# Two Winograd products of each SwiGLU pair in matmuls of 512 columns, and later operands for the last product

## The chip, the cores and the metric

The kernel runs on one core of one Trainium2 chip. The time is the device time of one execution in microseconds, as the median of several runs. Engines are named as in the profile: PE is TensorE's matmul, PEld its weight load, DVE VectorE, ACT ScalarE, POOL GpSimd, SP SyncE (which issues most DMAs).

## The reference

A decoder block on x of 512 tokens by 1024, in float32: two token mixers side by side, a sigmoid-gated merge, and a SwiGLU channel mixer with D_FF = 2816.

```
h  = rmsnorm(x, norm1_g);  z = h @ w_in + b_in
ya = conformer_conv(z) @ conv_w_out + conv_b_out
yb = (rg_lru(z) * gelu(z_rg)) @ lru_w_out
x  = x + (sigmoid(z_ga)*ya + sigmoid(z_gb)*yb) @ w_mix_out
h  = rmsnorm(x, norm2_g)
x  = x + (silu(h @ ffn_w1) * (h @ ffn_w3)) @ ffn_w2
out = rmsnorm(x, norm_f_g)
```

The change lies in the line before the last.

## The kernel before, in words

Every float32 operand of a large product is split into a high and a low part (`split`: ACT casts the high part, L123, DVE or POOL subtracts it from the original, L119). A product then is three matmuls: high weights by high tokens, high by low, low by high. A tile is 128 partitions by 512 columns.

The FFN's first two matrices run in 11 pairs k of 128-row blocks of D_FF (k and k + 11). Pair 0 is computed plainly; for pairs 1 to 10 the 2×2 blocks (block of D_FF by block of D_MODEL, by half of the tokens) go through a seven-product form of Winograd's: b11, t1, b21, t2, t4, b22 and t3. Each product is one call of `f_product` (L1082): for w1 and then w3 (`HALVES[i]` of one PSUM bank), for four blocks c, the three matmuls of 256 token columns, so 24 matmuls. The token operands stand in `f_in` (a11, s1 and so on, each as a pair of high and low parts of 256 columns), the weights in chunks of 128x1024 (`hl_fb`, `hl_ft` in the profile: plain blocks and sums). `ffn_product` calls it and combines: b11 goes into bank `fa`, which ACT copies to `fb` (L1182), b21 then accumulates into `fb` and t2 into `fa`; t1 goes into bank `fe` of another pool, which ACT copies to the tile `se` (L1187) and DVE adds after b22 and t3 (L906). `f_out` makes silu(w1 part) times w3 part (L1147, L1148) into the tiles `ou` and `ov`. The t1, t2, t3 sums of weights are made on DVE (L357, L119), t4's by an accumulating DMA of POOL (L355). The first two b11/b21 products of pairs 1 to 4 run earlier (`FIRST`, `NEXT`).

`F_ORDER` sets the order of the products, and with it the order in which weight chunks are loaded and split; `weights` works four chunks ahead of PE (`AHEAD`), with five buffers of split weights and four of raw ones. Within that a scheduler fixes the order of the instructions on each engine when the program is built.

The last product (w2, `Sevenfold` with name "o", tiles `or`, L953) has the same form in 512-column matmuls. `pair(k)` prepares its token operands from `ou` and `ov` of pair k: a split of u (`ous`), a sum s1 and its split (`os1p`), and two more operands, `oe` and the overwritten `ov`. `run` has a first part (products r1, r2, r5 over all k), in which `oe` and `ov` are also split (`oeb`, `ovb`), a second part (r7, r1 and r3 over all k), and a third part. At the end of the first part DVE adds the finished products to the residual (`plus`, tiles `x2b`). `SUMS_FROM` sets from which t4 on `pair` is called inside the FFN: with 5, after t4 of pairs 5 to 10, for pairs 0 to 5.

Of the kernel before, what the change touches and what calls it, by code (L numbers as in the profile page):

```python
# [8 lines left out]
F32 = mybir.dt.float32  # L9
F32R = mybir.dt.float32r  # L10
AF = mybir.ActivationFunctionType
# [21 lines left out]
SLOTS, SHORT, GATES = 59, 5, 6  # L33
# [11 lines left out]
PLAIN, FIRST, NEXT = 0, (1, 2), (3, 4)  # L45
BEGUN = FIRST + NEXT
ADDING = ()
SUMS_FROM, SUMS_AHEAD = 5, 3
GATES_AT = 6
SEED_AT = 4  # L50
SUMS_AT, SUMS_STEP, SUMS_LAG, STORE_LAG = 4, 3, 2, 4


# [33 lines left out]
def tile_block(ctx, tc, a, out):  # L87
    nc = tc.nc
# [12 lines left out]
    longt, shortt, gatet = tiles("long", SLOTS), tiles("short", SHORT), tiles("gate", GATES)  # L101
# [5 lines left out]
    def bank(name):  # L107
        return psum.tile([P, T], F32, tag="mm", name=name)

    def bank2(name):  # L110
        return psum2.tile([P, T], F32, tag="cv", name=name)

    vec, act, pe, pool_e = nc.vector, nc.scalar, nc.tensor, nc.gpsimd
# [4 lines left out]
    def sub(eng, o, x, y):  # L118
        return eng.tensor_tensor(out=o, in0=x, in1=y, op=ALU.subtract)  # L119
# [13 lines left out]
    def split(name, full, eng, p_=None, copy=act.copy):  # L133
        p_ = p_ or pairt(name)
        return split_to(*p_, full, eng, copy)[:2]
# [48 lines left out]
    def weights(key, ahead=AHEAD):  # L184
        i = next(i for i, c in enumerate(chunks) if c[0] == key)
        emit_to(i + 1 + ahead)
        return held.pop(key)
# [144 lines left out]
    KF = NF // 2  # L332
# [70 lines left out]
    F_PAIRS = [k for k in range(KF) if k != PLAIN]  # L403
    F_ORDER = []
    for k, before in zip(F_PAIRS, [None] + F_PAIRS):
# [2 lines left out]
            F_ORDER.append(("t4", before))  # L408
        F_ORDER += [("b22", k), ("t3", k)]
    F_ORDER.append(("t4", F_PAIRS[-1]))  # L410
    for n, k in F_ORDER:
        f_chunk(n, k)
    outq = Quartered("o", a["ffn_w2"][0].rearrange("(k p) n -> p k n", p=P), NF // 2, vec)
# [78 lines left out]
    eps_t = consts.tile([P, 1], F32, name="eps_t")  # L492
    vec.memset(eps_t, EPS)
    warm = consts.tile([P, 1], F32, name="warm")
# [102 lines left out]
    HALVES = [slice(0, 256), slice(256, 512)]  # L597
# [293 lines left out]
    for j in range(8):  # L891
        ws = w_tiles(f"lo{j}_0", 5) + w_tiles(f"lo{j}_1", 5)
        ps = bank(f"yb{j}")
# [12 lines left out]
    add = lambda o, x, y: vec.tensor_tensor(out=o, in0=x, in1=y, op=ALU.add)  # L906
    LO, HI = HALVES
# [7 lines left out]

    class Sevenfold:
        def __init__(self, q):
            self.q, self.uv, self.ops = q, {}, {}
            self.name, self.kh = q.name, q.kh

        def tile(self, j, make):
# [9 lines left out]
        def pair(self, k):  # L931

            n = self.name
            if k in self.ops:
                return
            ua, va = self.uv[k]
            u_ = split(f"{n}us{k}", ua, vec)
            s1 = shortt(f"{n}s1{k}")[:, LO]
            add(s1, va[:, LO], va[:, HI])
            sp = longt(f"{n}s1p{k}", F32R)  # L940
            split_to(sp[:, LO], sp[:, HI], s1, vec)
            e = (gatet if n == "o" and k < GATES else longt)(f"{n}e{k}")
            sub(vec, e[:, HI], ua[:, LO], va[:, LO])
            sub(vec, va[:, LO], s1, ua[:, LO])
            sub(vec, e[:, LO], ua[:, HI], va[:, LO])
            self.ops[k] = u_, sp, e, va

        def product(self, banks, i, x_, w_, start, stop, again=False):

# [5 lines left out]
        def run(self, sums, begun, end):  # L955

            n, kh, get = self.name, self.kh, self.q.get  # L960
            quarter = lambda p_, cs: tuple(v[:, cs] for v in p_)
            plus = lambda t, h, b_: add(sums[t][h], b_, sums[t][h])
            late = []
            r1, r2, r5 = ([bank(f"{n}{r}{i}") for i in range(2)] for r in ("r1", "r2", "r5"))
            for k in range(kh):
                for kk in range(min(kh, k + 1 + SUMS_AHEAD)):
                    self.pair(kk)
                wb21, wb11, wt1 = get(k, "b21", "b11", "t1")
                u_, sp, e, va = self.ops[k]
                todo = [(r1, quarter(u_, LO), wb11), (r2, quarter(u_, HI), wb21), (r5, (sp[:, LO], sp[:, HI]), wt1)]  # L970
                ends = k == kh - 1
                order = [(r, i) for i in range(2) for r in (0, 1)] + [(2, 0), (2, 1)] if ends else [(r, i) for r in range(3) for i in range(2)]
                for r, i in order:
                    self.product(todo[r][0], i, *todo[r][1:], k == 0, ends)
                    if ends and r == 1:
                        plus(i, 0, r1[i])
                        plus(i, 0, r2[i])
                late.append((split(f"{n}eb{k}", e, vec), split(f"{n}vb{k}", va, vec)))
                if k == 0:
                    begun()  # L980
            r2, r7 = [bank(f"{n}r3{i}") for i in range(2)], [bank2(f"{n}r7{i}") for i in range(2)]

            def second(k, wb22, wt2, wt3):
                e, va = late[k]
                todo = [(r7, quarter(e, HI), wt3), (r1, quarter(va, LO), wt2), (r2, quarter(e, LO), wb22)]
                ends = k == kh - 1
                order = [(r, i) for i in range(2) for r in (1, 2)] + [(0, 0), (0, 1)] if ends else [(r, i) for r in range(3) for i in range(2)]
                for r, i in order:
                    self.product(todo[r][0], i, *todo[r][1:], r != 1 and k == 0, ends, r == 1)

            def third(i, ks, cols=None):
                for dst, cs in cols or [(r1[i], slice(0, T))]:
                    for k in ks:
                        (wh, wl), = get(k, "t4")
                        self.product({i: dst}, i, quarter(late[k][1], HI), (wh[:, cs], wl[:, cs]), False, k == kh - 1, True)

            for k in range(kh - 1):
                second(k, *get(k, "b22", "t2", "t3"))
                if k == 0:
                    for i in range(2):  # L1000
                        plus(i, 1, r5[i])
                        plus(2 + i, 1, r5[i])

            act.activation(warm, late[-1][1][0][:, :1].bitcast(F32), AF.Sqrt, scale=0.0, bias=eps_t)
            last = get(kh - 1, "b22", "t2", "t3", ahead=AHEAD - 1)
            end(lambda: second(kh - 1, *last), plus, r1, r2, r7, third)

    m7 = Sevenfold(mixq)
    for n, j in enumerate(mixq.order()):
        ws = w_tiles(f"co{j}", ND)  # L1010
        ps = bank(f"ya{j}")
        mm3(ps, ws, un)
        o = sga[j]
# [56 lines left out]
    o7 = Sevenfold(outq)  # L1070
# [5 lines left out]
    def f_product(ps, k, x_, w_, again=False, ahead=AHEAD):  # L1076

        h, l = weights(f"f{w_}_{k}", ahead)
        for i in range(2):
            for c, (xh, xl) in enumerate(x_):  # L1080
                for m, (lw, rx_) in enumerate(((h, xh), (h, xl), (l, xh))):
                    pe.matmul(  # L1082
                        ps[:, HALVES[i]], lw[:, 4 * i + c, :], rx_, start=not (again or i or c or m),
                        stop=bool(i and c == 3 and m == 2), skip_group_check=True,
                    )

    first = {}
    for k in FIRST:
# [11 lines left out]
    with tc.manual_schedule(engines={ET.PE}):  # L1100
        ws = w_tiles(f"f1_{PLAIN}", ND, 0)
        for q in range(4):
            cs, ks = HALVES[q // 2], range(4 * (q % 2), 4 * (q % 2) + 4)
# [60 lines left out]
    for k in NEXT:  # L1164
        f_product(first[k][1], k, f_in["a12"], "b21", True)
        o7.uv[k] = longt(f"ou{k}"), longt(f"ov{k}")
        f_out(first[k][1], o7.uv[k][0][:, LO])

    seven = {}

    def ffn_product(n, k):

        b_ = seven.setdefault(k, {"a": first[k][0]} if k in BEGUN else {})
        x_ = {"b11": "a11", "b21": "a12", "b22": "s4", "t1": "s1", "t2": "s2", "t3": "s3", "t4": "a22"}[n]
        r = {"b11": "a", "b21": "b", "b22": "a", "t1": "e", "t2": "a", "t3": "c", "t4": "c"}[n]
        if n in ("b11", "t1"):
            b_[r] = (bank2 if r == "e" else bank)(f"f{r}_{k}")
        ps = b_[r]
        f_product(ps, k, f_in[x_], n, n not in ("b11", "t1"))
        if n in ("b11", "t2"):  # L1180
            new = b_["b" if n == "b11" else "c"] = bank(f"f{n}_{k}")
            act.copy(new, ps)  # L1182
            if n == "b11":
                o7.uv[k] = longt(f"ou{k}"), longt(f"ov{k}")
        elif n == "t1":
            b_["se"] = shortt(f"se_{k}")
            act.copy(b_["se"], ps)  # L1187
        elif n == "b22":
            add(ps, ps, b_["se"])
        elif n == "t3":  # L1190
            newest["added"] = add(b_["se"], ps, b_["se"]).ins
        if n not in ("b11", "t1", "t2"):
            i, cs = {"b21": (0, LO), "b22": (0, HI), "t3": (1, HI), "t4": (1, LO)}[n]
            f_out(b_["se"] if n == "t3" else ps, o7.uv[k][i][:, cs], -1.0 if n in ("b22", "t3") else 1.0)
        if n == "t4" and k >= SUMS_FROM:
            o7.pair(k - SUMS_FROM)

    for n, k in F_ORDER:
        ffn_product(n, k)

    x2 = [[longt(f"x2b{t}{h}") for h in range(2)] for t in range(NT)]
# [100 lines left out]
```

## Time and profile before

| | |
|---|---|
| runs | 797.24, 797.38, 797.41 us; median 797.38 |
| profiled execution | 797.4 us, span 795.6 us |
| granted TensorE clock | 1.0 |
| PE busy | 789.3 us (99%), 4378 matmuls |
| DVE busy | 673.9 us (85%) |
| ACT busy | 472.2 us (59%) |
| POOL busy | 229.2 us (29%) |

Times are in microseconds from the start of the span. Busy shares are shares of the span; the duration that a row gives for a matmul reaches into the next one, so the rate is read from start to start, or from the chain of work that ended last. The FFN's seven-product stage reaches from about 480 to 686 us, the last product from there to 790 us.

### The profile page before, as it was taken

To read this page: it belongs to the slowest core of one execution; us is meant where nothing else is said; L and a number is where in the kernel's file an instruction comes from. 1 tells how busy PE (TensorE), PEld (TensorE's weight loads), DVE (VectorE), ACT (ScalarE), POOL (GpSimd) and SP (SyncE) were. 2 spreads that over 40 slices of the span, in tenths; PEclk is the share of its full clock that TensorE was granted. 3 is DMA by queue.
4 is the path that set the end of the run, shared out by engine and by line. 5 is a ranking of instruction groups with operands and counts; after the bars stand their busy time and mean duration, and the time that the engine had idled before them with its cause. 6 is when DMAs were issued, how large, how long until landed. Compare 5 with 4: busy or idle time off the path is not lost.

```text
span 795.6 us, 12203 instructions
## 1 busy us (share of the span) xinstructions
PE 789.3 (99%) x4378; PEld 691.2 (87%) x4378; DVE 673.9 (85%) x1024; ACT 472.2 (59%) x686; POOL 229.2 (29%) x181
## 2 busy tenths in 40 slices
PE   9999999999999999999999999999999999999997
PEld 8888888888888888888888898999999999888886
DVE  6699899999989988786887889978878887889757
ACT  6646585988768855563335475545555555577434
POOL 1855766797666855130000000000000000000000
PEclk9999999999999999999999999999999999999999
DMA  6944647487555664468947545567555553676652
GB/s 204 259 137 144 192 138 209 121 243 211 169 172 172 206 189 120 129 201 278 280 140 245 172 134 158 129 170 188 152 133 133 133 133 106 202 269 204 195 176 106
DMA packets 184604, 140.29 MB, mean 176 GB/s; under 512 B 14259, under 2 KB 162143, under 8 KB 184543
## 3 DMA queue, kind: packets, MB, share of 16 engines
q1 hardware_dynamic: 183103, 134.27, 55.8%
q0 software_dynamic: 1440, 5.24, 3.5%
q8 instruction: 34, 0.56, 0.3%
q14 instruction: 27, 0.22, 0.1%
HBM read 113.79 MB, written 18.64 MB: 166 GB/s over the span
## 4 chain that ended last, share of the span: by engine, by line
PE 98%; DVE 1%; issue 0%; ACT 0%; ACTq 0%
PE z L534 36%; PE or L953 12%; PE ft L1082 7%; PE yb L534 7%; PE fa L1082 7%; PE fr L1082 6%; PE ya L534 5%; PE mxr L953 5%; PE fe L1082 4%; PE g L827 3%; PE fb L1082 2%; PE f L534 2%; PE warm L506 1%; PE f L1108 1%; PE tx L574 1%; PE th L574 0%
## 5 line engine op out<-in xcount | busy, mean ns | idle before, releaser
L702 DVE SCALAR_TENSOR_TENSOR cv<-u,par,cv 128x511 f32<-128x511 f32 (+19 forms) x240 | 162.6, 733 | 5.7 <-ACT cv L699 5.4
L119 POOL TENSOR_TENSOR hl_in<-raw_in,hl_in 128x1024 fp32r<-128x1024 f32 x51 | 123.6, 2427 | 82.9 <-ACT hl_in L123 69.4
L355 POOL DMA_DIRECT2D raw_fb<-raw_fb x10 | 8.7, 875 | 298.3 <-DVE raw_fb L357 186.2
L119 POOL TENSOR_TENSOR ows<-ows 128x256 f32<-128x256 f32 x66 | 57.0, 866 | 37.4 <-DMA ows<-in_ffn_w_dram 34.4
L123 ACT CAST hl_ft<-raw_fb 128x1024 fp32r<-128x1024 f32 x40 | 41.9, 1049 | 32.1 <-DVE raw_fb L357 16.6
L123 ACT CAST hl_in<-raw_in 128x1024 fp32r<-128x1024 f32 x50 | 52.1, 1043 | 11.2 <-PE z L534 6.6
L119 DVE TENSOR_TENSOR hl_ft<-raw_fb,hl_ft 128x1024 fp32r<-128x1024 f32 x40 | 48.6, 1221 | 6.6 <-ACT hl_ft L123 6.5
L119 DVE TENSOR_TENSOR hl_fb<-raw_fb,hl_fb 128x1024 fp32r<-128x1024 f32 x30 | 36.6, 1222 | 9.4 <-ACT hl_fb L123 9.2
L357 DVE TENSOR_TENSOR raw_fb<-raw_fb,raw_fb 128x1024 f32<-128x1024 f32 x20 | 24.5, 1225 | 20.9 <-DMA raw_fb<-in_ffn_w_dram 20.5
L534 PE MATMUL z<-h10h,hl_in 128*128 128x512 f32 (+1 forms) x108 | 41.5, 385 | 0.0
L534 PE MATMUL z<-h17h,hl_in 128*128 128x512 f32 (+1 forms) x108 | 41.1, 381 | 0.0
L534 PE MATMUL z<-h13h,hl_in 128*128 128x512 f32 (+1 forms) x108 | 41.1, 381 | 0.0
L534 PE MATMUL z<-h15h,hl_in 128*128 128x512 f32 (+1 forms) x108 | 41.1, 381 | 0.0
L534 PE MATMUL z<-h14h,hl_in 128*128 128x512 f32 (+1 forms) x108 | 41.1, 381 | 0.0
L534 PE MATMUL z<-h16h,hl_in 128*128 128x512 f32 (+1 forms) x108 | 41.1, 381 | 0.0
L534 PE MATMUL z<-h12h,hl_in 128*128 128x512 f32 (+1 forms) x108 | 41.1, 381 | 0.0
L534 PE MATMUL z<-h11h,hl_in 128*128 128x512 f32 (+1 forms) x108 | 41.1, 381 | 0.0
L123 ACT CAST hl_fb<-raw_fb 128x1024 fp32r<-128x1024 f32 x30 | 31.4, 1047 | 8.6 <-PE mxr L953 3.7
L119 DVE TENSOR_TENSOR hl_ob<-raw_ob,hl_ob 128x1024 fp32r<-128x1024 f32 (+1 forms) x23 | 27.1, 1178 | 9.8 <-ACT hl_ob L123 7.0
L123 ACT CAST hl_ob<-raw_ob 128x1024 fp32r<-128x1024 f32 (+1 forms) x23 | 23.3, 1014 | 19.9 <-PE or L953 12.6
L123 ACT CAST hl_ot<-raw_ot 128x1024 fp32r<-128x1024 f32 (+1 forms) x17 | 17.5, 1029 | 22.9 <-PE or L953 13.2
L1082 PE MATMUL fe<-hs_0h,hl_ft 128*128 128x256 f32 x160 | 30.8, 284 | 0.0
(1038 smaller groups left out, 2628.7 us busy)
## 6 DMA issues: line engine op xcount, KB each, us to landing
raw_in<-in_w_in_dram SPq DMA_DIRECT2D x52, 512.0 KB
raw_fb<-in_ffn_w_dram SPq DMA_DIRECT2D x96, 256.0 KB
ows<-in_ffn_w_dram SPq DMA_DIRECT2D x44, 256.0 KB
os<-ows SPq DMA_DIRECT2D x22, 512.0 KB
raw_ob<-in_ffn_w_dram SPq DMA_DIRECT2D x33, 256.0 KB
raw_ot<-os SPq DMA_DIRECT2D x33, 256.0 KB
raw_lo<-in_lru_w_out_dram SPq DMA_DIRECT2D x16, 320.0 KB
raw_fb<-raw_fb POOLq DMA_DIRECT2D x10, 512.0 KB, 4.6
```

The costliest lines, as they stand in the source:

```text
L119: return eng.tensor_tensor(out=o, in0=x, in1=y, op=ALU.subtract)
L123: copy(h, full)
L355: pool_e.dma_start(out=q, in_=y, accum_op=ALU.add)
L357: vec.tensor_tensor(out=q, in0=q, in1=y, op=ALU.add)
L506: pe.matmul(wp[:, :P], ones, ones, start=True, stop=True)
L534: pe.matmul(ps, l, r, start=i == 0, stop=i == n - 1)
L574: pe.transpose(ps[:, t * P : (t + 1) * P], src, ident)
L702: vec.scalar_tensor_tensor(out=acc[c][:, s:], in0=u[c][:, : T - s], scalar=dw(c, s), in1=acc[c][:, s:], op0=ALU.mult, op1=ALU.add)
L827: pe.matmul(ps, l, r, start=k == 0, stop=k == len(mms) - 1)
L953: pe.matmul(banks[i], l_[:, ts], r_, start=start and n == 0, stop=stop and n == 2, skip_group_check=again)
L1082: pe.matmul(ps[:, HALVES[i]], lw[:, 4 * i + c, :], rx_, start=not (again or i or c or m), stop=bool(i and c == 3 and m == 2), skip_group_c ...
L1108: pe.matmul(plain_1[:, cs], l, r, start=k == 0 and m == 0, stop=k == ND - 1 and m == 2)
```

## The change

Three things are changed.

First, t1 of pairs 3 to 10 and b11 of pairs 5 to 10 go through the new `f_wide`. It uses the high weights once for high and low tokens side by side (a matmul of 512 columns), and the low weights for the high tokens (256 columns, into the first half of the same bank). w1 and w3 have a bank each, and their two halves are added afterwards: ACT copies the first half to SBUF, DVE adds the second half from PSUM. For b11 the sum goes into bank `fa` and is then copied to `fb` as before. The side-by-side token tiles are made by 16 DMAs of 128 KB from SBUF to SBUF on SP's queue, eight for s1 ahead of the loop and eight for a11 ahead of t2 of pair 3.

Second, in `F_ORDER` b11 of pair k (5 to 10) stands ahead of t3 of pair k − 1, and not behind it.

Third, for the last product `SUMS_FROM` is 7 (pairs 0 to 3 are prepared in the FFN); from pair 4 on the two operands `oe` and `ov` are made by `others` only when they are split, and that is in the second part, two k ahead (`LATE_FIRST`, `LATE_AHEAD`).

```diff
-SUMS_FROM, SUMS_AHEAD = 5, 3
+SUMS_FROM, SUMS_AHEAD = 7, 3
+LATE_FIRST, LATE_AHEAD = 4, 2
...
+    for k in F_PAIRS:
+        if k not in BEGUN:
+            F_ORDER.remove(("b11", k))
+            F_ORDER.insert(F_ORDER.index(("t3", k - 1)), ("b11", k))
...
+            self.ops[k] = u_, sp
+            if n != "o" or k < KF - SUMS_FROM:
+                self.others(k)
+
+        def others(self, k):
+
+            if k in self.rest:
+                return
+            ua, va = self.uv[k]
+            e = (gatet if self.name == "o" and k < GATES else longt)(f"{self.name}e{k}")
             sub(vec, e[:, HI], ua[:, LO], va[:, LO])
-            sub(vec, va[:, LO], s1, ua[:, LO])
+            sub(vec, va[:, LO], va[:, HI], e[:, HI])
             sub(vec, e[:, LO], ua[:, HI], va[:, LO])
-            self.ops[k] = u_, sp, e, va
+            self.rest[k] = e, va
...
-                late.append((split(f"{n}eb{k}", e, vec), split(f"{n}vb{k}", va, vec)))
+                split_late([k] if k < LATE_FIRST else [])
...
             def second(k, wb22, wt2, wt3):
+                split_late(range(k + 1 + LATE_AHEAD))
...
-            act.activation(warm, late[-1][1][0][:, :1].bitcast(F32), AF.Sqrt, scale=0.0, bias=eps_t)
+            act.activation(warm, late[LATE_FIRST - 1][1][0][:, :1].bitcast(F32), AF.Sqrt, scale=0.0, bias=eps_t)
...
+    def f_wide(banks, k, x_, both_, w_):
+
+        h, l = weights(f"f{w_}_{k}")
+        for i, ps in enumerate(banks):
+            for c, (xh, _) in enumerate(x_):
+                pe.matmul(ps, h[:, 4 * i + c, :], both_[c], start=c == 0, stop=False, skip_group_check=True)
+                pe.matmul(ps[:, LO], l[:, 4 * i + c, :], xh, start=False, stop=c == 3, skip_group_check=True)
...
+    def side_by_side(n):
+        f_both[n] = [longt(f"{n}b{c}", F32R) for c in range(4)]
+        for both_, parts_ in zip(f_both[n], f_in[n]):
+            for cs, v in zip(HALVES, parts_):
+                nc.sync.dma_start(both_[:, cs].bitcast(F32), v.bitcast(F32))
+
+    side_by_side("s1")
...
+        if n == "t1" and k not in FIRST:
+            wide = [bank2(f"fe{i}_{k}") for i in range(2)]
+            f_wide(wide, k, f_in[x_], f_both[x_], n)
+            b_["se"] = shortt(f"se_{k}")
+            for cs, ps in zip(HALVES, wide):
+                act.copy(b_["se"][:, cs], ps[:, LO])
+                add(b_["se"][:, cs], ps[:, HI], b_["se"][:, cs])
+            return
+        if n == "b11":
+            wide = [bank(f"fa{i}_{k}") for i in range(2)]
+            f_wide(wide, k, f_in[x_], f_both[x_], n)
+            half = shortt(f"fh_{k}")
+            b_["a"], b_["b"] = bank(f"fa_{k}"), bank(f"fb_{k}")
+            for cs, ps in zip(HALVES, wide):
+                act.copy(half[:, cs], ps[:, LO])
+                add(b_["a"][:, cs], ps[:, HI], half[:, cs])
+            act.copy(b_["b"], b_["a"])
+            o7.uv[k] = longt(f"ou{k}"), longt(f"ov{k}")
+            return
...
     for n, k in F_ORDER:
+        if (n, k) == ("t2", NEXT[0]):
+            side_by_side("a11")
         ffn_product(n, k)
```

Three places show how the instructions move. The names are tile names with the pair's number and a buffer number. On DVE, between the t1 of pair 5 and the following products, there stood before:

```order
L906 TENSOR_TENSOR fr1_4_4774<-fr1_4_4774,se_4_5367 128x512
L119 TENSOR_TENSOR hl_ft2_5_5475<-raw_fb12_5_5372,hl_ft2_5_5475 128x1024
L1148 TENSOR_SCALAR ou4_4863<-fr1_4_4774,sl_5472 128x256
L906 TENSOR_TENSOR se_4_5367<-ft2_4_5402,se_4_5367 128x512
L119 TENSOR_TENSOR oe3_6633<-ou3_4831,ov3_4832 128x256
L119 TENSOR_TENSOR hl_ft4_4_5507<-raw_fb21_4_5211,hl_ft4_4_5507 128x1024
```

and at the same place stand now (`fa0_5` and `fa1_5` are the two wide banks of b11, `fh_5` holds the copied first halves):

```order
L911 TENSOR_TENSOR fr1_4_4774<-fr1_4_4774,se_4_5386 128x512
L120 TENSOR_TENSOR hl_ft2_5_5493<-raw_fb12_5_5364,hl_ft2_5_5493 128x1024
L1179 TENSOR_SCALAR ou4_4863<-fr1_4_4774,sl_5488 128x256
L911 TENSOR_TENSOR fa_5_5513<-fa0_5_5491,fh_5_5512 128x256
L120 TENSOR_TENSOR oe3_6940<-ou3_4831,ov3_4832 128x256
L911 TENSOR_TENSOR fa_5_5513<-fa1_5_5492,fh_5_5512 128x256
L120 TENSOR_TENSOR hl_ft4_4_5522<-raw_fb21_4_5231,hl_ft4_4_5522 128x1024
L911 TENSOR_TENSOR se_4_5386<-ft2_4_5418,se_4_5386 128x512
```

The two adds of b11 have come in behind `ou4`, and the add after t3 of pair 4 (`se_4`) now stands behind them. On ACT, in the same stretch of the changed kernel:

```order
L1178 ACTIVATE sl_5488<-fr1_4_4774 128x256
L1231 COPY fh_5_5512<-fa0_5_5491 128x256
L1231 COPY fh_5_5512<-fa1_5_5492 128x256
L124 COPY hl_ft4_4_5522<-raw_fb21_4_5231 128x1024
L1233 COPY fb_5_5514<-fa_5_5513 128x512
```

where the copies of the first halves stand ahead of the split of t4's weights, and the copy to `fb` behind it. On PE, at the start of the last product's second part, there stood before:

```order
L953 MATMUL or71_7469<-hl_ot2_1_7427,oeb1l_7073 128x512
L953 MATMUL or70_7468<-hl_ot2_2_7473,oeb2h_7110 128x512
L953 MATMUL or71_7469<-hl_ot2_2_7473,oeb2h_7110 128x512
L953 MATMUL or10_6994<-hl_ot2_0_7395,ovb0h_7034 128x512 x2
L953 MATMUL or10_6994<-hl_ot2_0_7395,ovb0l_7035 128x512
L953 MATMUL or10_6994<-hl_ot2_1_7427,ovb1h_7076 128x512 x2
```

and now:

```order
L967 MATMUL or70_7370<-hl_ot2_0_7313,oeb0h_6990 128x512 x2
L967 MATMUL or70_7370<-hl_ot2_0_7313,oeb0l_6991 128x512
L967 MATMUL or71_7371<-hl_ot2_0_7313,oeb0h_6990 128x512 x2
L967 MATMUL or71_7371<-hl_ot2_0_7313,oeb0l_6991 128x512
L967 MATMUL or10_6954<-hl_ot2_0_7313,ovb0h_6994 128x512 x2
L967 MATMUL or10_6954<-hl_ot2_0_7313,ovb0l_6995 128x512
L967 MATMUL or11_6955<-hl_ot2_0_7313,ovb0h_6994 128x512 x2
```

PE used to run k = 0, 1 and the beginning of 2 of the product r7 first, and now takes the three products of k = 0 one after the other; `or10`, which goes on accumulating in a bank of the first part, comes after 6 matmuls instead of 14.

More of the change, by code (lines that the diff above doesn't have):

```diff
@@ L917, in __init__ @@
         def __init__(self, q):
-            self.q, self.uv, self.ops = q, {}, {}
+            self.q, self.uv, self.ops, self.rest = q, {}, {}, {}
             self.name, self.kh = q.name, q.kh
@@ L941, in pair @@
             split_to(sp[:, LO], sp[:, HI], s1, vec)
-            e = (gatet if n == "o" and k < GATES else longt)(f"{n}e{k}")
+            self.ops[k] = u_, sp
[6 more added lines that the diff above has]
+            e = (gatet if self.name == "o" and k < GATES else longt)(f"{self.name}e{k}")
             sub(vec, e[:, HI], ua[:, LO], va[:, LO])
-            sub(vec, va[:, LO], s1, ua[:, LO])
+            sub(vec, va[:, LO], va[:, HI], e[:, HI])
             sub(vec, e[:, LO], ua[:, HI], va[:, LO])
-            self.ops[k] = u_, sp, e, va
+            self.rest[k] = e, va
         def product(self, banks, i, x_, w_, start, stop, again=False):
@@ L962, in run, with split_late @@
             plus = lambda t, h, b_: add(sums[t][h], b_, sums[t][h])
-            late = []
+            late = {}
+            def split_late(ks):
+                for k in ks:
+                    if k < kh and k not in late:
+                        self.others(k)
+                        e, va = self.rest[k]
+                        late[k] = split(f"{n}eb{k}", e, vec), split(f"{n}vb{k}", va, vec)
             r1, r2, r5 = ([bank(f"{n}{r}{i}") for i in range(2)] for r in ("r1", "r2", "r5"))
@@ L968, in run @@
                 wb21, wb11, wt1 = get(k, "b21", "b11", "t1")
-                u_, sp, e, va = self.ops[k]
+                u_, sp = self.ops[k]
                 todo = [(r1, quarter(u_, LO), wb11), (r2, quarter(u_, HI), wb21), (r5, (sp[:, LO], sp[:, HI]), wt1)]
@@ L1167, in tile_block @@
         f_out(first[k][1], o7.uv[k][0][:, LO])
+    f_both = {}
+    def side_by_side(n):
[4 more added lines that the diff above has]
+    side_by_side("s1")
     seven = {}
@@ L1175, in ffn_product @@
         r = {"b11": "a", "b21": "b", "b22": "a", "t1": "e", "t2": "a", "t3": "c", "t4": "c"}[n]
-        if n in ("b11", "t1"):
+        if n == "t1" and k not in FIRST:
[17 more added lines that the diff above has]
+            return
+        if n == "t1":
             b_[r] = (bank2 if r == "e" else bank)(f"f{r}_{k}")
         ps = b_[r]
[L1179 to L1184, printed above, removed]
+        f_product(ps, k, f_in[x_], n, n != "t1")
+        if n == "t2":
+            b_["c"] = bank(f"f{n}_{k}")
+            act.copy(b_["c"], ps)
         elif n == "t1":
@@ L1191, in ffn_product @@
             newest["added"] = add(b_["se"], ps, b_["se"]).ins
-        if n not in ("b11", "t1", "t2"):
+        if n not in ("t1", "t2"):
             i, cs = {"b21": (0, LO), "b22": (0, HI), "t3": (1, HI), "t4": (1, LO)}[n]
```

## The prediction

> **What bounds the kernel now.** I read the page's busy times first, then its chain of work that ended last.
>
> ```profile
> span 795.6 us, 12203 instructions
> PE 789.3 (99%) x4378; PEld 691.2 (87%) x4378; DVE 673.9 (85%) x1024; ACT 472.2 (59%) x686; POOL 229.2 (29%) x181
> PE 98%; DVE 1%; issue 0%; ACT 0%; ACTq 0%
> ```
>
> TensorE is busy for 99% of the span and makes 98% of the chain. So a change can pay only by giving PE less time, or by removing one of its few gaps; any new wait of PE is paid in full. The profiled execution took 797.4 us (span 795.6 and 1.8 around it), the median of the runs is 797.38, so the sum is made on 797.4. A measurement of this kernel tells about 0.2% from no change, 1.59 us; faster means under 795.79, slower over 798.97.
>
> Next, the chain in order of time, in the FFN around pair 5 (t3_4, b11_5, t1_5, b21_5) and in the one long stretch of 512-column matmuls. Columns: start, us, what.
>
> ```profile
> 558.15 2.88 PE ft L1082 x24
> 561.03 2.88 PE fa L1082 x24
> 563.91 2.88 PE fe L1082 x24
> 566.79 2.88 PE fb L1082 x24
> ...
> 375.31 43.52 PE ya L534 x192
> ```
>
> A product of 24 matmuls of 256 columns takes 2.88 us, 120.0 ns each. A 512-column matmul takes 43.52/192 = 226.7 ns, less than two of the short ones (240.0). Twice the difference of 106.7 ns for 256 columns leaves 13.3 ns per matmul that does not depend on its width.
>
> The last view is the table of busy time by windows (us: PE, PEld, DVE, ACT, POOL, then clock, DMA share, GB/s).
>
> ```profile
> 540.00:560.00 20.00, 20.00 (x169) 20.00 (x168) 17.31 (x21) 10.81 (x15) 0.86 (x1) 1.00 0.61 162
> 680.00:700.00 20.00, 20.00 (x108) 17.18 (x107) 15.40 (x24) 11.19 (x18) 0.00 (x0) 1.00 0.73 249
> 700.00:720.00 20.00, 20.00 (x90) 16.53 (x89) 19.93 (x35) 15.59 (x25) 0.00 (x0) 1.00 0.64 217
> 720.00:740.00 20.00, 20.00 (x89) 16.21 (x88) 20.00 (x31) 15.00 (x21) 0.00 (x0) 1.00 0.60 188
> ```
>
> The granted clock is 1.00 in all of them. VectorE has 2.7 us in 20 free in the FFN, and none from 700 to 740 in the last product.
>
> **The change, part by part.** *Wide products.* A triple of three 256-column matmuls (3 × 120.0 = 360.0 ns) becomes one of 512 and one of 256 columns (226.7 + 120.0 = 346.7 ns). That is 13.3 ns for each of 8 triples, 0.107 us a product; eight t1 and six b11 give 112 triples and **−1.49 us**, all on PE and so on the path.
>
> Does mixing widths cost something? Near the end of the trace PE goes from 512 to 256 columns with operands long ready:
>
> ```profile
> 787.82 0.39 PE L953 MATMUL or<-hl_ot,ovb10l 128*128 128x512 f32 x1
> 788.04 0.40 PE L953 MATMUL last<-hl_ot,ovb8h 128*128 128x256 f32 x2
> 788.28 0.28 PE L953 MATMUL last<-hl_ot,ovb8l 128*128 128x256 f32 x1
> ```
>
> From start to start, 0.22 us for the last 512 and 0.24 for two 256s: an even flow to the printed 0.01. An error of 0.005 us per pair on 112 pairs is 0.5 us, so the term lies between −1.0 and −2.0; I take −1.49.
>
> The 13.3 ns are what a rule speaks against. The Trainium skill, "TensorE: Matmul & The Clock Gate", section "Wait — 56ns, not 53.3ns?", gives a fixed cost of about 2.5 ns per matmul on a warm array. By that rule 112 matmuls fewer are worth 0.28 us, and the sum would be 1.2 us higher. Rows of this trace disagree with it for these matmuls (120.0 and 226.7 ns), and the measurement decides.
>
> *What the wide products add elsewhere.* The two halves have to be added. Per pair that is four DVE adds of 128x256 out of PSUM, and on ACT two 256 copies more for b11, and two 256 copies in place of one of 512 for t1. The nearest rows, of the same window:
>
> ```profile
> 622.55 0.69 DVE L906 TENSOR_TENSOR se<-ft,se 128x512 f32<-128x512 f32 x1
> 623.15 0.42 DVE L1148 SCALAR_TENSOR_TENSOR ou<-fa,sl 128x256 f32<-128x256 f32 x1
> 623.48 1.22 DVE L119 TENSOR_TENSOR hl_ft<-raw_fb,hl_ft 128x1024 fp32r<-128x1024 f32 x1
> ```
>
> A 256 operation holds the queue 0.33 us (623.15 to 623.48), so DVE gets 1.33 us a pair, which the 2.7 us free in 20 cover. If that cover is gone, it is the price of the weight loop's rival below. t1's sum is read only by b22's add, four products later, so its longer chain is hidden. b11's is less so: b21 accumulates into bank fb, a copy of the new sum.
>
> *The reorder* pays for that: b11 now runs one product earlier, t3 and t1 (2.88 + 2.77 us) stand between it and b21. I take pair 5, the first with a wide b11, for the tightest, since a11's copies are issued just ahead of its weights. The work there on DVE and ACT:
>
> ```profile
> 560.98 0.69 DVE L906 TENSOR_TENSOR fr<-fr,se 128x512 f32<-128x512 f32 x1
> 561.58 1.22 DVE L119 TENSOR_TENSOR hl_ft<-raw_fb,hl_ft 128x1024 fp32r<-128x1024 f32 x1
> 562.71 0.42 DVE L1148 SCALAR_TENSOR_TENSOR ou<-fr,sl 128x256 f32<-128x256 f32 x1
> 563.04 0.68 DVE L906 TENSOR_TENSOR se<-ft,se 128x512 f32<-128x512 f32 x1
> 561.77 0.38 ACT L1147 ACTIVATE sl<-fr 128x256 f32<-128x256 f32 x1 [2.15 <-DVE fr L906]
> 564.15 0.58 ACT L1182 COPY fb<-fa 128x512 f32<-128x512 f32 x1
> ```
>
> Behind `ou` (free at 563.04) come the first b11 add, the e-subtraction and the second add, 3 × 0.33; pair 4's two wide-t1 adds ahead of them push all by 0.66: the sum is ready at 564.7, its copy (0.58) at 565.3. b21_5 starts at 566.79 − 0.21 (two t1 already shorter) − 0.11 − 0.11 = 566.4. That leaves **1.1 us**. It can be eaten by the side-by-side copies: 1 MB for a11 on SP's queue ahead of pair 5's weights. From the window 680 to 700 all 16 engines move 249/0.73 = 341 GB/s, so the copies take 3.1 us of them; if every weight came 3.1 us later, PE would stand 3.1 − 1.1 = 2.0 us. The DVE row that takes those weights has already waited:
>
> ```profile
> 552.23 1.23 DVE L357 TENSOR_TENSOR raw_fb<-raw_fb,raw_fb 128x1024 f32<-128x1024 f32 x1 [2.55 <-DMA raw_fb<-in_ffn_w_dram]
> ```
>
> so delays do reach DVE there. Bounds 0 to 2.0 us; nearer to 0, since the window is only 0.61 full: I book **+0.1**. The copies of s1 stand in an earlier stretch with no such chain behind them: 0 to 1, taken as nothing. From pair 6 on, the PE order repeats with more lead and I book nothing.
>
> *Later operands of the last product.* Per pair the e and v splits are two 512 operations of 0.60 us (560.98 to 561.58) and three 256 subtractions, 2.2 us. For seven pairs they leave the first part or the FFN for the second part; pairs 4 and 5 bring the first part their u-split, sum and s1-split, 0.60 + 2 × 0.33 each. So 700 to 740, which is full, gets lighter by some 7 × 1.2 + 5 × 1.0 − 2.6 = 11 us. In the second part a k needs 2.2 and one and a half weight splits of 1.14 (561.58 to 562.71), 3.9 us of DVE against 18 × 226.7 ns = 4.08 us of PE. Pairs 4 and 5 are split before that part begins and pair 6 right behind its first eight adds, some 20 us before PE reads it, so nothing is booked. The other joint is the first part's pair 4, whose u-split stands behind this weight split now:
>
> ```profile
> 698.39 1.23 DVE L119 TENSOR_TENSOR hl_ob<-raw_ob,hl_ob 128x1024 fp32r<-128x1024 f32 x1 [2.81 <-DMA x2b<-x2k]
> 685.91 14.31 PE or L953 x63
> ```
>
> It is ready at 698.39 + 1.14 + 0.69 = 700.2; PE starts the last product at 685.9 and needs it four k later, at 702.2. 2 us are left, and nothing is booked; the bound is 1.
>
> The gain: at the start of the second part PE today waits for DVE, which is backed up.
>
> ```profile
> 732.47 0.61 PE L953 MATMUL or<-hl_ot,oeb2h 128*128 128x512 f32 x2
> 732.97 0.73 PE L953 MATMUL or<-hl_ot,ovb0h 128*128 128x512 f32 x2
> 733.53 0.39 PE L953 MATMUL or<-hl_ot,ovb0l 128*128 128x512 f32 x1
> 732.21 0.70 DVE L906 TENSOR_TENSOR x2b<-or,x2b 128x512 f32<-128x512 f32 x1
> PEld or L953 <- DVE x2b L906: 0.5, 2, 0.3
> ```
>
> 732.47 to 733.53 holds four matmuls, 0.91 us at 226.7 ns, and takes 1.06. With DVE ahead the adds come in time: **−0.15**, bounds −0.15 and +0.5 (PE now reaches the first of these adds after 6 matmuls, not 14).
>
> Sum: −1.49 + 0.1 − 0.15 = −1.54, from 797.4 **795.9 us**.
>
> **The rivals.** *Forecast* (0.66): PE is shorter and never waits. Own range 795.2 to 796.4.
>
> *A wait at the joints* (0.17). b21_5 waits for the copied sum, or the second part for its operands, 0.8 to 2.0 us in all: 796.5 to 797.7, no change. For it: 1.1 us of slack against copies worth 3.1 us. Against: the DMA window is 0.61 full. The Trainium skill, "DMA: Bandwidth & Descriptors", section "Issuing engines are not separate DMA queues", says that transfers share the same 16 engines whoever starts them, which would not let the copies run past the weights; no run here shows it yet.
>
> *The weight loop becomes the bound: slower* (0.12). A pair takes 7 × 2.88 = 20.2 us, and DVE stands still in it for
>
> ```profile
> 605.83 1.23 DVE L119 TENSOR_TENSOR hl_fb<-raw_fb,hl_fb 128x1024 fp32r<-128x1024 f32 x1 [0.62 <-ACT hl_fb L123]
> 609.59 1.23 DVE L357 TENSOR_TENSOR raw_fb<-raw_fb,raw_fb 128x1024 f32<-128x1024 f32 x1 [2.54 <-DMA raw_fb<-in_ffn_w_dram]
> 620.20 0.86 POOL L355 DMA_DIRECT2D raw_fb<-raw_fb  x1 [19.31 <-DVE hl_fb L119]
> ```
>
> 3.2 us, most of it for loads into buffers that DVE, through POOL's accumulation, itself sets free. If these waits do not shrink, the 1.33 us added lengthen the pair. Six pairs × 1.33 = 8.0 us, less 0.2 kept from pairs 3 and 4: 805.2 at worst; half of it 801.2. It turns the result slower from 0.3 us per pair. Against: the weights are split four chunks ahead of PE, so a late DVE first eats lead.
>
> *Alternating widths cost* (0.05). The only place where PE alternates shows a dear 256 between 512s:
>
> ```profile
> 477.27 0.47 PE f L534 x2
> 477.74 0.20 PE f L1108
> 477.94 0.23 PE f L534
> 477.10 0.40 ACT L123 CAST h26h<-hf 128x256 fp32r<-128x256 f32 x1
> ```
>
> 0.20 instead of 0.12. 112 × 0.08 = 9.0 us, less nothing: 806.4. Against: its operand h26h was still being written until 477.50, so the weight load was late and could not hide.
>
> **How the numbers follow.** The forecast's 0.66 lies on both sides of 795.79: 0.38 faster, 0.28 within; the joints add 0.17 to the latter (0.45); the two others are slower, 0.17. The range leaves out these two but for their edge, and 0.03 below 795.2: 795.2 to 799.0.
>
> **What would show it.** Right: PE's chain rows for fe from pair 3 and fa from pair 5 of 2.77 us, no PE wait on `fb` or `fa`, DVE's DMA wait per pair down by about 1.3 us, and the 700 to 740 windows under 20.00. Wrong: fe rows near 3.5 us (alternation); a gap ahead of fb near 566 (joint); a pair of over 20.2 us with unchanged DMA waits (loop); DVE still full past 740 and PE waiting for `oeb` or `ovb`.

## The result and the profile after

The changed kernel takes 799.1 us as a median of 16 runs (797.1 to 800.98) against 797.39 (796.98 to 798.16, also 16) for the kernel before: 1.71 us or 0.21% more by the medians; the ratio of the comparison is 1.0018, 95% interval 1.0011 to 1.0025. Forecast were 795.9 us and a range up to 799.0. Two things stand in this: the time is higher, and it scatters over 4 us where it scattered over 1.2.

The profiled execution is the shortest of the 16, 797.1 us. Its page begins with the busy times and the chain:

```profile
span 795.3 us, 12045 instructions
PE 788.1 (99%) x4266; PEld 684.2 (86%) x4266; DVE 684.5 (86%) x1052; ACT 475.7 (60%) x706; POOL 228.0 (29%) x181
PE 88%; DVE 6%; DMA 3%; ACT 1%; issue 1%; SPq 1%; ACTq 0%; DVEq 0%; POOLq 0%
```

112 matmuls are gone and PE is busy for 1.2 us less, but the chain holds 88% of PE and not 98%: DMAs, DVE and SP's queue have come into it. The chain in order of time shows where, on the way to b21 of pair 5 (start, us, what):

```profile
552.75 4.34 DMA raw_fb<-in_ffn_w_dram
...
563.22 0.61 DVE fr L911
563.83 1.12 DVE hl_ft L120
564.95 0.34 DVE ou L1179
565.28 0.34 DVE fa L911
565.87 0.43 DVE fa L911
566.33 0.58 ACT fb L1233
566.95 3.15 PE fb L1105 x24
```

This is the chain that the prediction walked: `fr`, `hl_ft`, `ou`, the two adds of b11, the copy to `fb`. The copy was to end at 565.3 and ends at 566.9, 1.6 us later than worked out there; PE waits, and from here back to about 489 us the chain lies on the weights and not on PE. The timeline of PE gives the wait (its last column is the idle time and what ended it):

```profile
565.80 0.28 PE L1116 MATMUL fe<-hs_0h,hl_ft 128*128 128x256 f32 x1
566.95 0.39 PE L1105 MATMUL fb<-h24h,hl_fb 128*128 128x256 f32 x1 [0.87 <-ACT fb L1233]
567.17 0.28 PE L1105 MATMUL fb<-h24l,hl_fb 128*128 128x256 f32 x1
```

565.80 to 566.95 is 1.15 us, 1.03 more than a 256 matmul's 0.12, and the first matmul after a wait costs 0.1 more (0.22 to the next start). From pair 6 to pair 10 PE waits no more before the FFN's last product. Two steady pairs, before and after, from t1 of one pair to t1 of the next:

```profile
604.23 2.88 PE fe L1082 x24
624.39 2.88 PE fe L1082 x24
```

```profile
604.50 0.23 PE fe L1115
624.55 0.23 PE fe L1115
```

20.16 us became 20.05. The forecast was 0.21 less for the two wide products in it (a t1 and a b11); 0.11 is what came.

This profile explains an execution of 797.1 us. Further traces of the same kernel, taken later, show longer ones (e13 and e14 below).

### The profile page after: what moved, and what is told of

Its sections match the earlier page's. It is cut to its first block, busy times and chain, and to the rows that moved or that the text cites. A ratio compares the mean times of both kernels' runs of the same rounds, so it can differ in the third digit from the quotient of the medians.

```text
span 795.3 us, 12045 instructions
## 1 busy us (share of the span) xinstructions
PE 788.1 (99%) x4266; PEld 684.2 (86%) x4266; DVE 684.5 (86%) x1052; ACT 475.7 (60%) x706; POOL 228.0 (29%) x181
## 4 chain that ended last, share of the span: by engine, by line
PE 88%; DVE 6%; DMA 3%; ACT 1%; issue 1%; SPq 1%; ACTq 0%; DVEq 0%; POOLq 0%
PE z L539 36%; PE or L967 12%; PE yb L539 7%; PE ya L539 5%; PE mxr L967 5%; PE ft L1105 5%; PE fa L1105 4%; PE g L832 3%; PE fb L1105 2%; DMA raw_fb<-in_ffn_w_dram 2%; DVE hl_ft L120 2%; PE fr L1105 1%; PE f L539 1%; PE fe L1115 1%; PE fa L1115 1%; DVE raw_fb L358 1%
## 5 line engine op out<-in xcount | busy, mean ns | idle before, releaser
L1105 PE MATMUL ft<-hs_1h,hl_ft 128*128 128x256 f32 x160 | 30.4, 283 | 0.0
```

What stands on the lines that cost most here:

```text
L1105: pe.matmul(ps[:, HALVES[i]], lw[:, 4 * i + c, :], rx_, start=not (again or i or c or m), stop=bool(i and c == 3 and m == 2), skip_group_c ...
```

## The experiments

Theories at the start: J, the joint ahead of b21 of pair 5; C, the copies as the reason why pair 5's weights come late there; L, the added work on DVE and ACT in every pair; R, the reorder or the late operands. The ratios are to the kernel before on the same chip beside each group of experiments (medians of 797.57 us beside e1 to e4, 797.48 beside e5 to e8, 797.51 beside e9 to e11).

**e1_again**: the changed kernel, no edit.

> The changed kernel once more, for a second trace. Theory J (joint: the sum of b11_5 comes too late for b21_5, because the weights of pair 5 come late): about 799, spread over 2 us, and the wait of PE ahead of fb of pair 5, 1.1 us in the first trace, is longer by about what the execution takes more than 797.1. Theory L (weight loop: the added DVE and ACT work lengthens every pair): the added time is spread over pairs 5 to 10.

798.06 us median of 10 (797.2 to 802.01), ratio 1.0015 (1.0001 to 1.0028). The traced execution was again a short one (797.2), with the same wait, 1.2 us from start to start ahead of `fb` of pair 5.

**e2_copies**: the kernel before, and the copies, read by nothing.

```
+    side_by_side("s1")
...
+        if (n, k) == ("t2", NEXT[0]):
+            side_by_side("a11")
```

> The kernel before with the 16 side-by-side copies issued at the places of the change, and nothing reading them. If the copies alone delay the weights enough to stop PE (theory C, a part of J): over 798, with a wider spread. If the kernel before has slack for them and the fault lies in the chain that the wide b11 lengthens (J without C): 797.3 to 797.6. Theory L: 797.4, no change.

798.25 us (797.57 to 799.6), ratio 1.0010 (1.0000 to 1.0019). By time the interval begins at no difference; the trace shows that 2 MB copied from SBUF to SBUF stop PE in a kernel that does not need them. The wait that PE had in the FFN:

```profile
PE fr L1082 <- ACT ft L1192: 0.7, 1, 0.7
```

That is b22 of pair 3, waiting for t2's copy `ft`. In the chain of the same trace:

```profile
534.60 3.43 DMA raw_fb<-in_ffn_w_dram
538.15 1.24 DVE raw_fb L357
539.46 1.05 ACT hl_ft L123
540.51 0.49 ACT ft L1192
541.05 3.13 PE fr L1082 x24
```

The weights of pair 4 land late, DVE's sum is late, ACT's split of it is late, and the copy that PE needs stands behind that split on ACT. So there is a second joint beside the one that I had looked at.

**e3_no_wide**: the change without wide products and copies.

```
+T1_WIDE, B11_WIDE = range(11, 11), range(11, 11)
...
-        if n == "t1" and k not in FIRST:
+        if n == "t1" and k in T1_WIDE:
...
-        if n == "b11":
+        if n == "b11" and k in B11_WIDE:
```

> The reorder of b11 and the later operands of the last product alone: no wide product, no copies. Theories J and L: 797.2 (0.15 us from the second part's start), spread as before. Theory R (the reorder itself or the later operands cost): 798 to 799.

797.37 us (796.97 to 797.6), ratio 0.9996 (0.9987 to 1.0006), scatter as small as before or smaller. R falls. The rows of the second part's start have no wait of PE any more, and 0.2 us by the medians is the size that was forecast, though the interval does not exclude nothing.

**e4_t1_only**: the kernel before with wide t1 and its copies.

> The kernel before with wide t1 and the s1 copies alone; b11, order and last product as before. Eight products less 0.107 us each: 796.5 if nothing waits. Theory J: 796.5 to 797.0, since b11's chain is the old one. Theory L: 797.5 or more, half of the added work being there.

799.1 us (797.05 to 799.88), ratio 1.0011 (1.0001 to 1.0020): J's 797.0 at most is missed. Its trace (797.89) has waits at two joints, neither of them b21's:

```profile
PE or L953 <- DVE x2b L906: 0.5, 1, 0.5
PE fr L1082 <- ACT ft L1208: 0.2, 1, 0.2
```

One is the start of the last product's second part, which the third part of the change had taken away, the other b22 of pair 3 again. With the s1 copies alone the median is as high as the change's; the kept execution is one of the shorter ones, and what lengthens those above 799 us no trace shows.

**e5_no_copies**: the change, reading existing 512-column tiles; the high-by-low terms are left out.

```
-                nc.sync.dma_start(both_[:, cs].bitcast(F32), v.bitcast(F32))
+        f_both[n] = f_high[n]
```

> The changed kernel without the 16 copies: the wide matmuls read existing 512-column tiles (the high parts alone, so the high-by-low terms are left out), everything else as in the change. Theory C (the copies delay pair 4's and 5's weights): no wait of PE at b21_5, the whole gain, 797.4 - 1.49 - 0.2 = 795.7, spread as before. Theory L (the added DVE and ACT work): 798 to 799 as with the copies.

796.73 us (796.26 to 797.28), ratio 0.9991 (0.9981 to 1.0000). Without the copies 1.3 us (against e1's median) to 2.4 us (against the first one) and the scatter are gone. But it is not 795.7: a wait of 0.2 us is left ahead of `fb` (0.4 from start to start), and the wide products themselves bring only half.

**e6_no_adds**: the change with the copies, without the added adds and ACT copies; the sums of the halves are left out.

```
+            act.copy(b_["se"], wide[1])
+            b_["a"], b_["b"] = wide[1], bank(f"fb_{k}")
```

> The changed kernel with the copies and the wide matmuls but without the added work on DVE and ACT: the sum of the two halves is left out, t1 is one ACT copy of 512 columns, b11 one copy from one of its banks. Theory C: the weights are still late by the copies; b11's chain is short again, so 796 to 798 with a wide spread. Theory L: 795.7, spread as before.

796.93 us (796.5 to 797.91), ratio 0.9995 (0.9986 to 1.0005). Its weights are as late as in the change (first sum of pair 5 in the table below), and b21 of pair 5 does not wait. That its shorter chain is the reason is an argument, but it fits e5: in this order of the products the copies and the adds share one slack, either alone nearly fits, and both do not. In the order of before, the copies alone do not fit either (e2).

**e7_later**: wide t1 from pair 6, wide b11 from pair 8, copies at t2 of pairs 5 and 6.

```
+T1_WIDE, B11_WIDE = range(6, 11), range(8, 11)
-        if (n, k) == ("t2", NEXT[0]):
+        if (n, k) == ("t2", 6):
             side_by_side("a11")
+        if (n, k) == ("t2", 5):
+            side_by_side("s1")
```

> The changed kernel with wide t1 from pair 6 and wide b11 from pair 8 only, and the copies issued at t2 of pairs 5 and 6, when the pairs take 7 products instead of 5 and the weight loop has slack. Theory C with J: 8 products less 0.107 and 0.2 from the last product, 796.4, spread as before. Theory L: each pair from 6 on still gets its added work, 797.5 or more.

796.74 us (796.08 to 798.48), ratio 0.9991 (0.9981 to 1.0000). The same copies and the same added work per pair, moved into pairs of seven products, cost nothing: no wait of PE in the FFN. L falls.

**e8_pool_copies**: the change with POOL's copies.

```
-                nc.sync.dma_start(both_[:, cs].bitcast(F32), v.bitcast(F32))
+                pool_e.tensor_copy(both_[:, cs], v.bitcast(F32))
```

> The changed kernel with the 16 copies made by POOL, idle there, in place of DMAs. Theory C: the weight loads keep their time, 795.7 to 796.2. If POOL's copies delay its accumulating DMAs, which stand in the same queue, or slow DVE, it is 797 or more. Theory L: 798 to 799.

797.53 us (796.93 to 798.68), ratio 1.0001 (0.9991 to 1.0010): better than the DMAs by 0.5 to 1.6 us, but in the trace the wait ahead of `fb` is still 0.5 us from start to start.

**e9_grouped**: e7_later with another order within a wide product.

```
+            for c in range(4):
+                pe.matmul(ps, h[:, 4 * i + c, :], both_[c], start=c == 0, stop=False, skip_group_check=True)
             for c, (xh, _) in enumerate(x_):
-                pe.matmul(ps, h[:, 4 * i + c, :], both_[c], start=c == 0, stop=False, skip_group_check=True)
                 pe.matmul(ps[:, LO], l[:, 4 * i + c, :], xh, start=False, stop=c == 3, skip_group_check=True)
```

> The kernel of e7_later with the wide product's matmuls in another order: per bank the four of 512 columns first, then the four of 256, so 4 changes of width per product and not 16. In the traces a wide product takes 2.83 us, not the 2.77 forecast: in a pair of one 512 and one 256 the 512 reads 233 to 241 ns. If the change of width costs (theory W): about 2.79 us a product, 8 products less 0.04 more than e7_later, 796.4. If a wide product costs 2.83 however it is ordered: 796.74 as e7_later.

796.8 us (796.58 to 798.01), ratio 0.9994 (0.9984 to 1.0003): by time it cannot be told from e7_later, the expected 0.3 us being below what ten runs tell. The traces tell it. PE's timeline of t1 of pair 9:

```profile
624.13 1.09 PE L1116 MATMUL fe<-s1b,hl_ft 128*128 128x512 f32 x4
625.06 0.63 PE L1118 MATMUL fe<-hs_0h,hl_ft 128*128 128x256 f32 x4
625.53 1.09 PE L1116 MATMUL fe<-s1b,hl_ft 128*128 128x512 f32 x4
626.46 0.64 PE L1118 MATMUL fe<-hs_0h,hl_ft 128*128 128x256 f32 x4
626.94 0.28 PE L1106 MATMUL fb<-h24h,hl_fb 128*128 128x256 f32 x1
```

The product takes 626.94 − 624.13 = 2.81 us, not 2.83. Four matmuls of 512 in a row take 0.93 us, 232 ns each, where the long stretch of 512s (`ya`) has 226.7. So it is not the change of width alone that costs: theory W explains 0.02 of the missing 0.05 us per product, and why a 512 takes 232 ns in this product stays open.

**e10_best**: grouped order, POOL's copies, wide t1 from pair 5, wide b11 from pair 6.

> Grouped order, copies by POOL, wide t1 from pair 5 and wide b11 from pair 6. By theories C, J and W: 11 products less about 0.09 each and 0.2 from the last product, 796.2, spread as before, no wait of PE in the FFN over 0.2 us. If the added DVE and ACT work costs in the steady pairs (theory L): 797 or more.

796.79 us (795.54 to 797.4), ratio 0.9989 (0.9979 to 0.9998), and the view of waits has none of PE in the FFN. Of the versions that leave nothing out it is the only one whose whole interval is below the kernel before (e7's ends at 1.0000), by 0.7 us in the medians; 796.2 was expected from 0.09 us a product, the traces give 0.07.

**e11_double**: the change with every copy issued twice, once into a tile that nothing reads.

```
+                nc.sync.dma_start(more[:, cs], v.bitcast(F32))
```

> The changed kernel with every side-by-side copy issued twice, the second one into a tile that nothing reads. Theory C: another 1 to 2.5 us, 800 to 801.5, with the wait at b21_5 grown by what the sum of t1's weights of pair 5 comes later. If the time does not hang on the copies: 798.5 to 799 as the change.

807.03 us (4 runs, 805.84 to 807.59), ratio 1.0123 (1.0106 to 1.0140): 8 us more than the change, three times the most that was expected. Its trace has these waits of PE in the FFN:

```profile
PE fr L1105 <- ACT ft L1244: 6.0, 2, 3.7
PE fb L1105 <- ACT fb L1235: 0.9, 1, 0.9
```

Both joints, b22 twice. And after the longest wait the clock falls (windows of 5 us, the value behind POOL's is the granted clock):

```profile
520.00:525.00 5.00, 5.00 (x44) 5.00 (x44) 0.66 (x2) 0.59 (x1) 0.00 (x0) 1.00 0.82 241
525.00:530.00 5.00, 1.35 (x10) 1.14 (x9) 2.22 (x2) 1.53 (x2) 0.00 (x0) 0.80 1.16 292
530.00:535.00 5.00, 5.00 (x26) 5.00 (x26) 4.93 (x6) 2.26 (x3) 0.86 (x1) 0.52 0.38 76
```

26 matmuls in 5 us where there were 44: while the clock is at 0.52 the trace's matmuls of 256 columns take 213 ns, 93 more, some 2.2 us on top of the wait.

**e12_trace, e13_trace, e14_trace**: the changed kernel three times more, to see its longer executions.

> A third trace of the changed kernel. If it is an execution of 798.5 or more, theory C with J expects its extra time as a wait of PE at a product that needs a copy standing on ACT behind a late weight split: b22 of pairs 2 to 4 (bank ft) or b21 of pair 5 (bank fb). Theory L expects it in the pairs from 6 on.

> A fourth trace of the changed kernel, with the same expectations as for the third: if it is a longer execution, C with J puts the extra wait at b22 of pairs 2 to 4 or at b21 of pair 5, L in the pairs from 6 on.

> A fifth trace of the changed kernel, with the same expectations as for the third: if it is a longer execution, C with J puts the extra wait at b22 of pairs 2 to 4 or at b21 of pair 5, L in the pairs from 6 on.

796.97, 799.38 and 799.15 us (one execution each). The last two are of the size of the median, and the chain of e14 shows what grew:

```profile
541.50 3.20 DMA a11b<-h22l
544.70 7.13 DMA raw_fb<-raw_fb
551.88 0.37 SPq L346
...
554.60 5.12 DMA raw_fb<-in_ffn_w_dram
...
568.43 0.58 ACT fb L1233
569.05 3.14 PE fb L1105 x24
```

The rows show the a11 copies, POOL's accumulating DMA (`raw_fb<-raw_fb`, t4's sum of pair 4) and, issued when that has landed, the load of pair 5's weights. The chain puts the start of POOL's DMA down to the copy that landed last before it, but DVE's t2 sum explains it in both kernels: the DMA follows its end by some 0.5 us (541.46 + 1.23 to 543.22 before, 542.94 + 1.22 to 544.70 in e14). So it starts 1.5 us later in e14, and it takes 2.0 us longer (issues from 536 to 560 us; KB each, us to landing; before and e14):

```profile
raw_fb<-raw_fb POOLq DMA_DIRECT2D x1, 512.0 KB, 5.1
```

```profile
raw_fb<-raw_fb POOLq DMA_DIRECT2D x1, 512.0 KB, 7.1
```

What moves beside it is for the most part not the copies. The queue that carries SP's DMAs (q1) moves 0.53 MB in these 7.1 us, against 0.06 MB in the 5.1 us before. That is the size of two weight loads, which SP now issues behind its copies (before and e14):

```profile
540.36 0.92 SPq L345 DMA_DIRECT2D raw_fb<-in_ffn_w_dram  x2
```

```profile
543.49 1.14 SPq L346 DMA_DIRECT2D raw_fb<-in_ffn_w_dram  x2
```

Nor are the 2.0 us all theirs: the same DMA takes 6.0 us in e3 and, in the row below, 5.7 in e5, both without any copy.

```profile
raw_fb<-raw_fb POOLq DMA_DIRECT2D x1, 512.0 KB, 5.7
```

SP is busy for 5.6 us with issuing the eight copies (537.77 to 543.38). Whether they delay the weights more by this or by the time of the DMA engines, no run separates, since e8 takes both away. PE's waits in e14 are the two joints again:

```profile
PE fb L1105 <- ACT fb L1233: 1.7, 1, 1.7
PE fr L1105 <- ACT ft L1242: 0.5, 1, 0.5
```

One measure orders most of the traces: the time on DVE from a sum that nothing of the change touches (pair 1's t2, near 497 us) to the first sum of pair 5. The rows of before (its second stands in the prediction), of the change, of e14 and of e7_later:

```profile
497.72 1.22 DVE L357 TENSOR_TENSOR raw_fb<-raw_fb,raw_fb 128x1024 f32<-128x1024 f32 x1
```

```profile
497.21 1.22 DVE L358 TENSOR_TENSOR raw_fb<-raw_fb,raw_fb 128x1024 f32<-128x1024 f32 x1
553.73 1.23 DVE L358 TENSOR_TENSOR raw_fb<-raw_fb,raw_fb 128x1024 f32<-128x1024 f32 x1 [3.81 <-DMA raw_fb<-in_ffn_w_dram]
```

```profile
497.75 1.22 DVE L358 TENSOR_TENSOR raw_fb<-raw_fb,raw_fb 128x1024 f32<-128x1024 f32 x1
555.83 1.23 DVE L358 TENSOR_TENSOR raw_fb<-raw_fb,raw_fb 128x1024 f32<-128x1024 f32 x1 [4.67 <-DMA raw_fb<-in_ffn_w_dram]
```

```profile
497.17 1.22 DVE L359 TENSOR_TENSOR raw_fb<-raw_fb,raw_fb 128x1024 f32<-128x1024 f32 x1
551.74 1.23 DVE L359 TENSOR_TENSOR raw_fb<-raw_fb,raw_fb 128x1024 f32<-128x1024 f32 x1 [2.87 <-DMA raw_fb<-in_ffn_w_dram]
```

| trace | sum to sum, us | what PE lost against an even flow at b22 of pairs 2 to 4 and b21 of pair 5, us |
|---|---|---|
| before | 54.5 | 0 |
| e7_later | 54.6 | 0 |
| e3_no_wide | 54.8 | 0 |
| e10_best | 55.1 | 0 |
| e9_grouped | 55.5 | 0 |
| e4_t1_only | 55.8 | 0.4 |
| e5_no_copies | 55.8 | 0.4 |
| e12 (change) | 56.0 | 0.6 |
| e8_pool_copies | 56.0 | 0.6 |
| e6_no_adds | 56.4 | 0.2 |
| after (change) | 56.5 | 1.1 |
| e1 (change) | 56.8 | 1.3 |
| e2_copies | 57.4 | 1.1 |
| e13 (change) | 57.6 | 2.3 |
| e14 (change) | 58.1 | 2.7 |
| e11_double | 65.4 | 10 |

In the five traces of the change, in e5, e8 and e11, PE loses what this stretch takes over some 55.4 us. Those with the old, shorter chain of b11 in pair 5 need not follow this: e6 and e2 lose less than that. The longer executions of the change differ from its short ones by these waits: e14's loss is 1.6 us above that of the first trace, its span 2.1 us longer; the other 0.5 lie ahead of the sum near 497 (497.75 against 497.21).

## Why the prediction was wrong, point by point

**Two terms were mis-sized. The first is the wide product.** Forecast: 0.107 us for each of 14, −1.49 in all, bounds −1.0 and −2.0. Measured: two steady pairs of starts give 20.16 − 20.05 = 0.11 for two, some 0.053 each, **−0.75** in all, outside my bounds. The step that failed is the price of the 512: I took the 226.7 ns of a stretch that holds nothing else. In the alternating product a pair takes 2.83/8 = 354 ns and not 346.7. That mixing could cost I had seen and reasoned away with a single change of width at the end of the trace; but there only one 512 followed by 256s is seen, and never a 512 behind a 256. The trace of before has that as well, where PE goes from the FFN to the last product:

```profile
685.74 0.40 PE L953 MATMUL or<-hl_ob,ous0h 128*128 128x512 f32 x1
685.98 0.40 PE L953 MATMUL or<-hl_ob,ous0l 128*128 128x512 f32 x1
```

From start to start that is 0.24 us and not 0.227. Some 0.01 us more for each of 112 pairs is over 1 us, so this row would have carried the upper bound near nothing. The rival of alternation had 80 ns a pair, far too much, so the truth lay between the two, where I had put nothing. The rule of about 2.5 ns per matmul from the Trainium skill, "TensorE: Matmul & The Clock Gate", section "Wait — 56ns, not 53.3ns?", would have made it −0.28; the measured term lies between that and mine, and for the plain products the rows still say 13.3 ns.

**The second, and the larger one for the median, is the joint: the right place with the wrong price.** I had 1.1 us of slack at b21 of pair 5, bounds 0 to 2.0, and booked 0.1; the five traces of the change lost 0.6 to 2.0 us there. The slack and the work on DVE and ACT behind `fr` came as worked out; what came late was its input: the sum of pair 5 stands 2.0 us later behind pair 1's (56.5 against 54.5), and 3.6 in e14. In the first trace 2.1 us (the copy's 1.6, and 0.5 because everything from the sum near 497 on lies that much earlier) less the slack of 1.1 is the wait of 1.0. That the window was "only 0.61 full" was the faulty reason: an average over 20 us says nothing of a load that waits for an accumulating DMA, which waits for a sum on DVE, which waits for earlier loads that the copies make late. The rule in the Trainium skill, "DMA: Bandwidth & Descriptors", section "Issuing engines are not separate DMA queues", that transfers interleave on the same 16 engines whoever starts them, agrees with e14: POOL's DMA took 5.1 us before and 7.1 beside SP's loads. How much of the 2.0 us is due to it is not shown, as e3 has 6.0 us without copies.

**A second joint was missing.** "The copies of s1 stand in an earlier stretch with no such chain behind them", with 0 to 1 us taken as nothing, was wrong: b22 of pairs 2 to 4 waits for t2's copy, which stands on ACT behind a weight split. e2 shows it with 0.7 us, e14 with 0.5, e11 with 6.0. In e14, 1.0 us of the delay stands already at the first sum of pair 3 (523.32 against 522.25), before any a11 copy is issued.

**Right were** the reorder and the late operands (e3: 797.37; −0.15 was forecast, no PE wait left at the second part's start; the time itself is within the noise), and that the added 1.33 us per pair vanish in DVE's waits once a pair has seven products: DVE's wait for pair 8's weights fell from 2.54 us (609.59) to 1.16.

```profile
608.67 1.23 DVE L358 TENSOR_TENSOR raw_fb<-raw_fb,raw_fb 128x1024 f32<-128x1024 f32 x1 [1.16 <-DMA raw_fb<-in_ffn_w_dram]
```

So the loop rival fails where it was placed, in the steady pairs. It holds where I had not put it: in pairs 1 to 4, whose b11 and b21 have been done earlier, so that PE takes 5 × 2.88 = 14.4 us a pair. In the trace of before the first sums of pairs 2 to 5 follow each other by 14 to 15.4 us: there the weights come no faster than PE uses them, and nothing lets them catch up.

**The sum as measured** is −0.75 (wide), −0.2 (second part, e3's medians) and +0.6 to +2.7 (joints, e12 to e14), which from 797.4 gives 797.1 to 799.2; the median of 799.1 is at the upper end, and e14 (799.15) is met. For e13 it gives 798.8, 0.6 too little. For the first trace, with 1.1 at the joint, it gives 797.6, and 797.1 was measured: there the stages ahead of the FFN account for the difference, since its mark on DVE stands at 497.21 and not 497.72.

## What to carry to other kernels

Cost a transfer not by the mean load of a window but by the chain that it delays: find the stretch in which supply and demand run at the same pace (here the pairs of five products), and put nothing extra there; the same copies and adds in the pairs of seven products were free. When two additions each fit into one slack, sum them against it before booking either at nothing. And take an instruction's price from a row where it stands among the same neighbours; where there is none, let the bounds reach to the value without any gain.

## What the hardware showed that was not expected

A 512-column matmul behind other widths took 232 ns in a row of four (e9) and some 236 alternating with 256s (the change), against 226.7 in a stretch of its own; the cause was not found. The same accumulating DMA of 512 KB took 5.1 us before, 5.7 and 6.0 in traces without copies (e5, e3) and up to 7.1 with them (e14), so its time alone does not tell what ran beside it. And a wait of PE of 3.8 us (e11) was followed by about 5 us at a granted clock of 0.52, so that it cost another 2.2 us, while one of 2.5 us in the same trace (to 563.14, clock 1.00 from 560 to 565) and one of 1.9 us in e14 were not followed by one. The Trainium skill, "TensorE: Matmul & The Clock Gate", section "What's actually happening", has the clock at half rate after an idle window of about 3.4 us: these three waits agree with it.
